# One layer of a hybrid diffusion backbone on one core: scans started one block later, one load per chunk, the gate arithmetic reordered

## The chip, the core and the metric

The kernel runs on one core of a Trainium2 chip: TensorE (PE) for matrix products, VectorE (DVE), ScalarE (ACT) and GpSimd (POOL) for elementwise work, SyncE (SP) as the queue that starts nearly all DMA transfers. Each engine takes its own instructions in order and waits on semaphores for the others. The metric is the device time of one execution in microseconds. Three runs of the kernel before took 1649.82, 1650.39 and 1653.24 us; the median is 1650.39.

## What is computed

The layer takes 1024 latent tokens and 256 context tokens of width 1024. A modulated norm feeds one wide input projection; from it come, for four retention heads and four mLSTM heads, a query, a key, a value and an output gate, further the mLSTM's scalar gates and two wide branch gates. Each head is scanned in both directions, in chunks of 128 tokens:

```python
# retention, one chunk
scores = jnp.einsum("bhld,bhsd->bhls", qc, kc) * intra
out = jnp.einsum("bhls,bhsv->bhlv", scores, vc) + inter[..., None] * jnp.einsum("bhld,bhdv->bhlv", qc, s)
s_new = chunk_decay[:, None, None] * s + jnp.einsum("bhsd,bhsv->bhdv", kc * to_end[..., None], vc)
...
# mLSTM, one chunk: b_cum is the running sum of log forget gates, ic the input gate
log_src = b_last[..., None] - b_cum + ic
m_new = jnp.maximum(b_last + m, jnp.max(log_src, axis=-1))
w_old = jnp.exp(b_last + m - m_new)
w_src = jnp.exp(log_src - m_new[..., None])
c_new = w_old[..., None, None] * c_mat + jnp.einsum("bhs,bhsv,bhsd->bhvd", w_src, vc, kc)
...
y_ret = from_heads(head_norm(ret)).astype(dtype) * jax.nn.silu(rg)
y_ml = from_heads(head_norm(jax.nn.sigmoid(to_heads(mo, ML_HEADS)) * ml)).astype(dtype)
merged = jax.nn.sigmoid(bg_ret) * (y_ret @ w_ret_up) + jax.nn.sigmoid(bg_ml) * (y_ml @ w_ml_up)
x = x + g1 * (merged @ w_out)
x = x + g2 * swiglu(modulate(rms_norm(x, norm2_gain[layer]), sh2, sc2), w_ffn_in[layer], w_ffn_out[layer])
```

All is float32; the kernel writes an operand of a large product as the sum of a high and a low part and adds three products.

## The kernel before

The program is one long pipeline on one core. The part that the change touches is the head section, from about 155 to 776 us of the span. It is a row of 22 blocks (`run_blocks`, L320): `u1p0` to `u7p1` (head u = 1 to 7; part 0 makes its key and value, part 1 its query and gate) and then `bg0` to `bg7` (the branch gates). Every block is a product of 256 by 1024 weights with all 1024 tokens in seven products of half size (`winograd_block`, L276), each of 12 matmuls of 128x512 (`prod`, L253, L258): 84 matmuls. The weights of a block are loaded (L211) and split into high (ACT, L191) and low (DVE, L192) parts one block ahead, after sums and differences on DVE and POOL (L230). Products collect in the PSUM tiles `ch` and `ts`; DVE (L288) or ACT (L286, L293) take them out; the finished tiles are rotated (L576 to L582), stored, or transposed by PE (L564). The first product of a block is issued ahead of the last two of the block before.

Beside the blocks run generators. `tick()` (L994) is called once per product, seven times a block; `beside(gen, rate)` (L1004) adds a generator that is advanced `rate` times per tick on average; `drain()` (L1007) runs all of them to their end. They are:

- `gates()` (L691): the mLSTM's scalar gates for all eight head directions in 36-row tiles `g`: a log-sigmoid by way of DRAM (L706 to L712), six running sums and maxima as DVE scans (L724, L725), sums and differences over 36x1280 elements (L736, L737 on POOL; L741, L747 on DVE), exponentials on ACT (L735, L750, L751), and 30 small PE transposes into `colq` (L768).
- `scan(u)` (L805), one per head. Its steps stand in numbered slots: `load` of a chunk's key and value `kv` from DRAM (L825), `decay` on POOL (L838), `advance` of the running state `sf` or `sb` (PE L852, DVE L857), `load_qk`, and for each of eight output chunks j `stage_a` (L887), `stage_b` (PE L898, DVE L901 or L903) and `stage_c` (PE L915 to L917 or L922 and L923, then ACT L918 or ACT and DVE L925 to L929, POOL L931, and a sum of squares on ACT, L933, whose elementwise result is thrown away in the tile `junk`). `norm_y` (L935) scales, `put_y` (L944) transposes by PE (L947) and stores. The four rotating PSUM buffers `sc` serve all of these.
- `ada2()` (L972): the second modulation vector from 64 loads of 256 KB with one DVE operation each (L983).
- `load_y_ret()` (L1059): loads the retention results for the stage after and splits them (L1069).

What Python issues first does not stand first in the end: a scheduler sets the order of instructions on each engine from the program and the buffers' waits. The rates, slots and buffer counts move it.

## Time and profile before

| what | value |
|---|---|
| median of three runs | 1650.39 us |
| profiled execution, its own time | 1655.51 us |
| its span, first to last instruction | 1653.7 us |
| PE busy | 1578.3 us, 95% |
| DVE busy | 1003.5 us, 61% |
| ACT busy | 725.7 us, 44% |
| POOL busy | 460.2 us, 28% |
| mean granted TensorE clock | 0.984 |

Busy shares are means over very different stages, and a matmul's recorded time covers its way through the array, so that two neighbours overlap. Within the head section a better measure is the length of a block: how long 84 matmuls and the scans' small ones took.

### The profile page before, as it was taken

What the parts mean: (1) busy time and instruction counts of PE and PEld (TensorE: products, weight loads), DVE (VectorE), ACT (ScalarE), POOL (GpSimd) and SP (SyncE); (2) the same over time, 40 slices, a digit from 0 to 9 for tenths busy, and PEclk for the clock granted to TensorE, in tenths of its full rate; (3) what the DMA queues carried; (4) which work ended last, traced back from release to release, by engine and by line L of the source; (5) the groups of instructions that cost most, each with busy time, mean ns of one, the idle gap of its engine ahead of it and who ended that gap; (6) DMA issues with size and microseconds to landing.
All of it is one profiled execution on the core that took longest, in us unless ns stands there. A gap on an engine that the chain in (4) does not pass through costs nothing.

```text
span 1653.7 us, 22635 instructions
## 1 busy us (share of the span) xinstructions
PE 1578.3 (95%) x7478; PEld 1287.9 (78%) x7478; DVE 1003.5 (61%) x1841; ACT 725.7 (44%) x1404; POOL 460.2 (28%) x506
## 2 busy tenths in 40 slices
PE   7999978899999999999999999999999999999997
PEld 2677757787878788778888777888888888888886
DVE  4578786776767767765445677555555555536243
ACT  4655434544545566655223354434443334534230
POOL 0143216455344444410220226222222221001001
PEclk9999978999999999999999999999999999999998
DMA  8753537787767765546456312222232224835531
GB/s 293 255 159 104 167 105 234 252 258 240 248 210 218 228 202 180 187 141 215 154 162 202 122 56 96 81 92 84 85 96 87 77 90 155 271 96 179 171 96 52
DMA packets 188230, 264.55 MB, mean 160 GB/s; under 512 B 19232, under 2 KB 85920, under 8 KB 188112
## 3 DMA queue, kind: packets, MB, share of 16 engines
q1 hardware_dynamic: 186240, 260.99, 49.8%
q10 hardware_dynamic: 1872, 2.10, 0.4%
q8 instruction: 59, 0.97, 0.2%
q14 instruction: 59, 0.48, 0.1%
HBM read 206.64 MB, written 56.38 MB: 159 GB/s over the span
## 4 chain that ended last, share of the span: by engine, by line
PE 51%; POOL 2%; DVE 2%; DMA 1%; ACT 1%; issue 0%; DVEq 0%; SPq 0%; ACTq 0%
PE ch L258 15%; PE ts L258 12%; PE ch L1291 2%; PE ch L1292 2%; PE ch L1290 2%; PE ts L1290 2%; PE ts L1292 2%; PE ts L1291 2%; POOL hid L1158 1%; PE ts L113 1%; PE ch L113 1%; PE ts L112 1%; PE ts L111 1%; PE ch L111 1%; PE ch L112 1%; POOL xf L396 1%
## 5 line engine op out<-in xcount | busy, mean ns | idle before, releaser
L192 DVE TENSOR_TENSOR fw<-raw,fw 128x512 fp32r<-128x512 f32 x305 | 223.1, 737 | 156.6 <-ACT fw L191 156.1
L258 PE MATMUL ts<-A,fw 128*128 128x512 f32 x1200 | 300.7, 398 | 1.8 <-DVE A L397 0.9
L191 ACT CAST fw<-raw 128x512 fp32r<-128x512 f32 x305 | 188.0, 620 | 257.2 <-PE ch L1292 89.0
L258 PE MATMUL ch<-A,fw 128*128 128x512 f32 x1176 | 289.4, 394 | 0.0
L258 PEld LDWEIGHTS ts<-A,fw 128*128 128x128 f32 x1200 | 225.1, 191 | 50.9 <-DVE A L397 3.0
L258 PE MATMUL ch<-t,fw 128*128 128x512 f32 x1008 | 250.4, 396 | 5.5 <-ACT u L293 3.9
L258 PEld LDWEIGHTS ch<-A,fw 128*128 128x128 f32 x1176 | 219.5, 189 | 45.8 <-issue 1.0
L258 PEld LDWEIGHTS ch<-t,fw 128*128 128x128 f32 x1008 | 187.5, 189 | 44.7 <-ACT u L293 5.1
L1158 POOL TENSOR_TENSOR hid<-hid,sg 128x512 f32<-128x512 f32 x44 | 90.2, 2062 | 217.6 <-DVE hid L288 200.9
L258 PE MATMUL ts<-t,fw 128*128 128x512 f32 x504 | 129.6, 404 | 3.2 <-ACT fw L191 1.9
L293 ACT COPY u<-ch 128x512 f32<-128x512 f32 x104 | 60.9, 586 | 134.0 <-PE ch L258 133.7
L258 PEld LDWEIGHTS ts<-t,fw 128*128 128x128 f32 x504 | 95.6, 193 | 23.1 <-ACT fw L191 2.1
L192 DVE TENSOR_TENSOR fw<-stg,fw 128x512 fp32r<-128x512 f32 x126 | 94.5, 750 | 31.3 <-ACT fw L191 31.2
L230 POOL TENSOR_TENSOR stg<-raw,raw 128x512 f32<-128x512 f32 x42 | 63.5, 1513 | 156.2 <-DVE fw L192 100.4
L191 ACT CAST fw<-stg 128x512 fp32r<-128x512 f32 x126 | 78.6, 624 | 59.4 <-DVE stg L230 29.2
L838 POOL TENSOR_SCALAR vs<-kv,dcol 128x128 f32<-128x128 f32 x72 | 63.0, 882 | 63.1 <-DMA kv<-kv_d 33.0
L838 POOL TENSOR_SCALAR vs<-kv,colq 128x129 f32<-128x129 f32 x72 | 54.8, 762 | 78.5 <-PE sc L852 38.0
L1282 POOL TENSOR_SCALAR cp<-cp,cpack 128x256 f32<-128x256 f32 (+1 forms) x6 | 8.2, 1361 | 222.1 <-ACT stg L1336 222.1
L192 DVE TENSOR_TENSOR fw<-s,fw 128x512 fp32r<-128x512 f32 x42 | 33.4, 796 | 48.0 <-ACT fw L191 48.0
L983 DVE SCALAR_TENSOR_TENSOR acc<-stg,silu_c,acc 128x512 f32<-128x512 f32 x56 | 46.8, 836 | 18.2 <-DMA stg<-wada 18.1
L230 DVE TENSOR_TENSOR stg<-raw,raw 128x512 f32<-128x512 f32 x42 | 39.0, 930 | 27.1 <-DMA raw<-wffn 16.8
L396 POOL TENSOR_SCALAR t<-stg,a,sh 128x512 f32<-128x512 f32 (+1 forms) x24 | 27.3, 1144 | 95.8 <-issue 31.5
(362 smaller groups left out, 2973.3 us busy)
## 6 DMA issues: line engine op xcount, KB each, us to landing
raw<-wffn SPq DMA_DIRECT2D x88, 256.0 KB
raw<-wfo SPq DMA_DIRECT2D x88, 256.0 KB
kv<-kv_d SPq DMA_DIRECT2D x152, 128.0 KB
raw<-win SPq DMA_DIRECT2D x64, 256.0 KB
stg<-wada SPq DMA_DIRECT2D x64, 256.0 KB
hid_d<-hid SPq DMA_DIRECT2D x44, 256.0 KB
hraw<-hid_d SPq DMA_DIRECT2D x40, 256.0 KB
araw<-wada SPq DMA_DIRECT2D x32, 256.0 KB
```

The costliest lines, as they stand in the source:

```text
L191: nc.scalar.copy(hi, x)
L192: nc.vector.tensor_tensor(out=lo, in0=x, in1=hi.bitcast(F32), op=ALU.subtract)
L230: eng.tensor_tensor(out=o, in0=x, in1=y, op=op)
L258: nc.tensor.matmul(ps, lhsT=w[wp_][:, c], rhs=x[xp][k], start=start and k == i == 0, stop=cont or (stop and k == 3 and i == 2), skip_group ...
L293: nc.scalar.copy(o, chain)
L396: nc.gpsimd.tensor_scalar(out=tmp, in0=xn, scalar1=scale, scalar2=shift, op0=ALU.mult, op1=ALU.add)
L838: nc.gpsimd.tensor_scalar(out=vs, in0=kv[d, n][1], scalar1=col, scalar2=None, op0=ALU.mult)
L983: nc.vector.scalar_tensor_tensor(out=acc, in0=raw, scalar=s, in1=acc, op0=ALU.mult, op1=ALU.add)
L1158: nc.gpsimd.tensor_tensor(out=c, in0=c, in1=sgs[f, hf], op=ALU.mult)
L1290: nc.tensor.matmul(ps, lhsT=w[0][:, c], rhs=h[0][:, t], start=kt == 0, stop=False)
L1291: nc.tensor.matmul(ps, lhsT=w[0][:, c], rhs=h[1][:, t], start=False, stop=False)
L1292: nc.tensor.matmul(ps, lhsT=w[1][:, c], rhs=h[0][:, t], start=False, stop=kt == 2 * NG - 1)
```

## The change

The generators get other starting places, rates and slots. `gates()` still starts with `u1p0`, now at rate 1.0 and with its steps spread over more yields: the forget gate is loaded and biased first, the log-sigmoid's three DMA trips have yields between them, and the two wide subtractions go from POOL to DVE. The drain, the opening of the scans' pool and `ada2` move from `u2p1` to `u3p0`; `ada2` runs at 0.68 in place of 0.95. `scan(u)` starts with the next head's part 0, at 1.5 slots per tick in place of 1.45, and the last one with `bg4` in place of `bg3`; `load_y_ret` starts with `bg7` at 1.6 in place of `bg6` at 1.0. In a scan each chunk of keys and values is loaded once for both directions (10 loads in place of 19, nine buffers in place of eight), most slots move back by one, `put_y` by two. The mask is loaded by each mLSTM scan into the buffer `dt`, and the sum of squares throws its elementwise result into the last quarter of the PSUM tile `po` in place of `junk`.

```diff
+        def load_rows(t, tl, c0):
+            for x, c in ((t, c0), (tl, c0 + H)):
+                nc.gpsimd.memset(x, 0.0)
+                for d in range(2):
+                    nc.sync.dma_start(x[32 * d:32 * d + H], e_d[c + 32 * d:c + 32 * d + H])
...
+        load_rows(gf, gfl, 64)
+        yield
+        load_rows(gi, gil, 0)
...
+        biased(1, gf, gfl)
         for d in range(2):
             nc.sync.dma_start(rows[0][4 * d:4 * d + H], gf[32 * d:32 * d + H])
         nc.sync.dma_start(lsx, ls_d[0])
         yield
-        log_sigmoid(pg, lso, lsx, [P, 80], "g")
...
+        biased(0, gi, gil)
...
+        yield
+        yield
+        yield
+        log_sigmoid(pg, lso, lsx, [P, 80], "g")
+        yield
...
                 nc.vector.tensor_tensor_scan(out=v(bb), data0=v(rm), data1=v(gf), initial=0.0, op0=ALU.mult, op1=ALU.add)
+                yield
                 nc.vector.tensor_tensor_scan(out=v(m), data0=v(gf), data1=v(gi), initial=m[r, 0:1] if i else 0.0,
                                              op0=ALU.add, op1=ALU.max)
-                yield
-        yield
+                if not (d and i == 0):
+                    yield
...
+        nc.scalar.activation(rm, m, AF.Exp, scale=-1.0)
+        nc.vector.tensor_tensor(out=gi, in0=gi, in1=bb, op=ALU.subtract)
...
+        nc.vector.tensor_tensor(out=bb, in0=bb, in1=m, op=ALU.subtract)
...
-        nc.gpsimd.tensor_tensor(out=gi, in0=gi, in1=bb, op=ALU.subtract)
-        nc.gpsimd.tensor_tensor(out=bb, in0=bb, in1=m, op=ALU.subtract)
...
-        def load(d, n):
-            t = bt([P, 2 * P + 1], "kv", 8)
+        def load(n):
+            t = bt([P, 2 * P + 1], "kv", 9)
...
-            return bt([P, P + 1], "sf", 3)[:, :W]
+            return bt([P, P + 1], "sf", 4)[:, :W]
...
+        for i, n in enumerate((0, 1, 9, 8, 7, 6, 5, 4, 3, 2)):
+            after(i // 2 if i < 9 else 6, load, n)
         for i, n in enumerate((1, 0, 9, 8, 7, 6, 5, 4, 3)):
-            after(i // 2, load, 1, n)
-            at(i // 2 + 2, decay, 1, n)
-            at(i // 2 + 3, advance, 1, n)
-        for n in range(NCH):
-            after(5 + n, load, 0, n)
-            if n < 9:
-                at(7 + n, decay, 0, n)
-                at(8 + n, advance, 0, n)
+            at(i // 2 + 3, decay, 1, n)
+            at(i // 2 + 4, advance, 1, n)
+        for n in range(9):
+            at(4 + n if n < 2 else 7 + n, decay, 0, n)
+            at(6 + n if n < 2 else 8 + n, advance, 0, n)
...
-            junk = bt([P, P], "junk", 1)
-            nc.scalar.activation(junk, raw, AF.Square, accum_out=ssq[:, j:j + 1])
+            nc.scalar.activation(po[:, 3 * P:], raw, AF.Square, accum_out=ssq[:, j:j + 1])
...
-            at(9 + j, stage_a, j)
-            at(10 + j, stage_b, j)
-            at(11 + j, stage_c, j)
-        at(20, norm_y)
-        at(23, put_y, 0)
-        at(24, put_y, 4)
+            at(10 + j, stage_a, j)
+            at(11 + j, stage_b, j)
+            at(12 + j, stage_c, j)
+        at(21, norm_y)
+        at(25, put_y, 0)
+        at(26, put_y, 4)
...
-                if part == 0:
+                if part == 1:
                     return
-                if u == 2:
+                if u == 1:
+                    beside(gates())
+                if u == 3:
                     drain()
                     es_g.close()
                     open_scans()
-                    beside(ada2(), 0.95)
-                if u >= 2:
-                    beside(scan(u - 2), 1.45)
+                    beside(ada2(), 0.68)
+                if u >= 3:
+                    beside(scan(u - 3), 1.5)
...
-                if blk in (1, 3):
-                    beside(scan(2 * H - 2 + blk // 2), 1.45)
-                if blk == 6:
+                if blk in (0, 2, 4):
+                    beside(scan(2 * H - 3 + blk // 2), 1.5)
+                if blk == 7:
                     drain()
                     es_b.close()
-                    beside(load_y_ret())
+                    beside(load_y_ret(), 1.6)
```

Three places show what the scheduler made of it. The first is DVE while `u2p0` runs, around the gate scans. Before, from the last low part of `u1p1` (`fw_1980`) on; `fw_2134` and `fw_2139` are the low parts of `u2p1`'s first two factors, `g` the gate tiles:

```order
L192 TENSOR_TENSOR fw_1980<-raw_1796,fw_1980 128x512
L192 TENSOR_TENSOR fw_2134<-raw_1983,fw_2134 128x512
L230 TENSOR_TENSOR stg_2137<-raw_1985,raw_1987 128x512
L230 TENSOR_TENSOR s_2142<-stg_2137,raw_1983 128x512
L192 TENSOR_TENSOR fw_2139<-stg_2137,fw_2139 128x512
L724 SCALAR_TENSOR_TENSOR g_1576<-g_1575,g_1574 4x1280
L725 SCALAR_TENSOR_TENSOR g_1573<-g_1574,g_1572 4x1280
L724 SCALAR_TENSOR_TENSOR g_1576<-g_1575,g_1574 4x256
L725 SCALAR_TENSOR_TENSOR g_1573<-g_1574,g_1572 4x256
```

The same place now, from behind the six scans (which stand directly above, L740 and L742) to `fw_2062`, the low part of `u2p1`'s first factor; `kt` are finished tiles of `u2p0`:

```order
L755 COPY gm_1549<-g_1543 4x1
L749 TENSOR_TENSOR g_1542<-g_1542,g_1546 36x1280
L756 COPY gm_1549<-g_1543 4x1
L757 COPY gm_1549<-g_1543 4x7
L753 TENSOR_TENSOR g_1546<-g_1546,g_1543 36x1280
L288 TENSOR_TENSOR kt_2027<-ts_2014,u_1916 128x512
L759 TENSOR_TENSOR g_1544<-g_1546,gm_1549 36x1280
L578 TENSOR_TENSOR kt_2027<-kt_2027,rp_2029 128x512
L288 TENSOR_TENSOR kt_2055<-ts_1978,wt_2053 128x512
L579 TENSOR_TENSOR kt_2027<-kt_2027,wt_2033 128x512
L764 COPY gm_1551<-g_1546 4x10 x2
L192 TENSOR_TENSOR fw_2062<-raw_1970,fw_2062 128x512
```

The scans stood behind the first two factors of the next block and now stand ahead of both, with the two subtractions among them.

The second place is PE at the end of `u2p0`. Before, the first gate transpose (L768) stands between the first and the second product of `u2p1`:

```order
L258 MATMUL ch_2155<-A_116,fw_2134 128x512 x2
L258 MATMUL ch_2155<-A_117,fw_2134 128x512
L258 MATMUL ch_2155<-A_116,fw_2134 128x512
L768 MATMUL sc_2071<-cpack,g_1572 128x36 [waits DMAHW2_49,DMAHW4_49,PE_49,Pool_49]
L258 MATMUL ts_2281<-t_1254,fw_2139 128x512 [waits DVE_49]
L258 MATMUL ts_2281<-t_1255,fw_2139 128x512
L258 MATMUL ts_2281<-t_1254,fw_2139 128x512
```

Now, at the same count of large matmuls: `fw_1967` belongs to `u2p0`'s last product, `kt_2055` is the tile that DVE makes above, and `ch_2083` is `u2p1`'s first product, of which two matmuls stand ahead:

```order
L258 MATMUL ch_1903<-A_118,fw_1967 128x512 [waits Activation_49]
L258 MATMUL ch_1903<-A_119,fw_1967 128x512
L258 MATMUL ch_1903<-A_118,fw_1967 128x512 [waits DVE_49]
L258 MATMUL ch_1903<-A_118,fw_1967 128x512
L258 MATMUL ch_1903<-A_119,fw_1967 128x512
L564 MATMUL sc_2098<-cpack,kt_2055 128x128 [waits DVE_49,PE_49]
L564 MATMUL sc_2098<-cpack,kt_2055 128x128 x3
L258 MATMUL ts_1978<-A_118,fw_1964 128x512
L258 MATMUL ts_1978<-A_119,fw_1964 128x512
L258 MATMUL ts_1978<-A_118,fw_1964 128x512 x2
L258 MATMUL ch_2083<-A_116,fw_2062 128x512 [waits DVE_49]
```

The wait for POOL's subtraction is gone from here; the gate transposes (now L782) follow 17 large matmuls and four small ones further on, and a transpose that waits for DVE's `kt_2055` and a matmul that waits for `fw_2062` stand in their place.

The third place is PE in the last mLSTM scan, at two slots in one tick. Before, in `bg4`:

```order
L852 MATMUL sc_7586<-vs_7551,kv_7464 128x129 [waits DMAHW2_49,PE_49,Pool_49]
L922 MATMUL sc_7591<-sf_7508,qs_7517 128x129 [waits DVE_49]
L258 MATMUL ch_7186<-A_118,fw_7303 128x512
L258 MATMUL ch_7186<-A_119,fw_7303 128x512
L923 MATMUL sc_7591<-kv_7444,W_7519 128x129 [waits DVE_49]
L922 MATMUL sc_7591<-sb_7218,qs_7517 128x129
```

Now, in `bg5`:

```order
L936 MATMUL sc_7516<-sf_7404,qs_7430 128x129 [waits DVE_49]
L937 MATMUL sc_7516<-kv_7242,W_7432 128x129 [waits DVE_49]
L936 MATMUL sc_7516<-sb_7121,qs_7430 128x129
L937 MATMUL sc_7516<-kv_7242,W_7432 128x129
L912 MATMUL sc_7529<-qk_7416 128x128 [waits DMAHW2_49,PE_49]
L867 MATMUL sc_7544<-vs_7514,kv_7157 128x129 [waits DVE_49,Pool_49]
L258 MATMUL ts_7592<-t_1254,fw_7370 128x512
L936 MATMUL sc_7549<-sf_7421,qs_7480 128x129 [waits Activation_49]
```

The state `sf_7508` was begun one slot's matmuls ahead of its reader, `sf_7404` now two; and the reader's PSUM buffer is now waited for on ACT.

## Rows read from the trace of the kernel before

**Rows 1.** The page's first part: busy us, share, instructions.
```profile
PE 1578.3 (95%) x7478; PEld 1287.9 (78%) x7478; DVE 1003.5 (61%) x1841; ACT 725.7 (44%) x1404; POOL 460.2 (28%) x506
```
**Rows 2.** Stretches: length, PE busy (matmuls), granted clock, DMA share, GB/s.
```profile
199.64:265.55 65.91, 53.04 (x235) 0.84 0.49 157
265.55:337.26 71.71, 63.31 (x337) 0.93 0.73 232
337.26:737.10 399.84, 380.52 (x2097) 1.00 0.67 210
737.10:756.14 19.04, 19.04 (x85) 1.00 0.64 206
...
424.05:450.37 26.32, 26.32 (x149) 1.00 0.88 278
```
**Rows 3.** PE's waits, 155.15 to 776 us: total us, times, longest.
```profile
PE sc L947 <- DVE o L941: 9.4, 5, 3.5
PE sc L768 <- POOL g L736: 8.9, 1, 8.9
PE sc L922 <- DVE sf L857: 4.7, 4, 2.6
PE sc L915 <- DVE sf L857: 3.6, 3, 1.4
PE sc L852 <- POOL vs L838: 2.6, 2, 2.2
...
PE sc L768 <- ACT g L751: 1.4, 1, 1.4
```
**Rows 4.** PE's waits from 337.26 us on.
```profile
PE sc L947 <- DVE o L941: 5.9, 4, 1.8
```
**Rows 5.** Stretches at low clock: length, busy PE, PEld, DVE, ACT, POOL, clock.
```profile
220.92:231.16 10.24, 5.44 (x13) 4.25 (x14) 10.17 (x10) 3.58 (x5) 7.03 (x3) 0.50 0.03 5
...
237.99:244.82 6.83, 6.83 (x31) 5.59 (x31) 3.23 (x5) 4.16 (x15) 0.00 (x0) 0.50 0.46 125
```
**Rows 6.** PE and POOL in order of time: start, us, what, idle before.
```profile
225.29 0.32 PE L768 MATMUL sc<-cpack,g 36*128 36x36 f32 x1 [8.91 <-POOL g L736]
225.32 2.91 POOL L737 TENSOR_TENSOR g<-g,g 36x1280 f32<-36x1280 f32 x1
```
**Rows 7.** DVE in order of time, in the same stretch.
```profile
211.05 2.81 DVE L724 TENSOR_TENSOR_SCAN g<-g,g 4x1280 f32<-4x1280 f32 x1 [0.23 <-DMA g<-ls_d]
...
222.61 2.65 DVE L732 COPY gm<-g 4x7 f32<-4x7 f32 x1
...
225.90 4.11 DVE L192 TENSOR_TENSOR fw<-s,fw 128x512 fp32r<-128x512 f32 x1
...
231.14 1.48 DVE L741 TENSOR_TENSOR g<-g,gm 36x1280 f32<-36x1280 f32 x1
```
**Rows 8.** The page's costliest groups: busy us, mean ns, idle before.
```profile
L192 DVE TENSOR_TENSOR fw<-raw,fw 128x512 fp32r<-128x512 f32 x305 | 223.1, 737 | 156.6 <-ACT fw L191 156.1
```
**Rows 9.** The gate bias (L703): durations ns, first and last start us.
```profile
L703 DVE SCALAR_TENSOR_TENSOR g<-g,gbias,g x2: 1537/1537/1537, 170.8 to 179.4; 36x1280 f32<-36x1280 f32 x2
```
**Rows 10.** Waits of SP's queue, 155.15 to 776 us: total us, times, longest.
```profile
SPq L825 <- PE sc L852: 22.2, 27, 1.8
...
SPq L758 <- POOL g L737: 14.3, 1, 14.3
```
**Rows 11.** ACT's and POOL's waits, 337 to 737 us.
```profile
ACT junk L933 <- POOL o L931: 17.3, 21, 1.9
...
POOL o L931 <- DVE o L929: 23.7, 15, 4.2
```
**Rows 12.** Durations ns min/median/max of L933 and L931.
```profile
L933 ACT ACTIVATE junk<-o x64: 293/311/323, 279.0 to 714.4; 128x128 f32<-128x128 f32 x64
L931 POOL TENSOR_TENSOR o<-o,g x32: 454/460/892, 511.8 to 713.9; 128x128 f32<-128x128 f32 x32
```
**Rows 13.** DMA issues: number and KB of each.
```profile
kv<-kv_d SPq DMA_DIRECT2D x152, 128.0 KB
```

More of the change, by code (lines that the diff above doesn't have):

```diff
@@ L695, in gates, with biased @@
         ls_d = [dram.tile([P, 80], F32, name=f"ls_d{i}") for i in range(2)]
-        for t in (gi, gil, gf, gfl, bb, mprev):
-            nc.gpsimd.memset(t, 0.0)
-        for t, c0 in ((gi, 0), (gil, H), (gf, 64), (gfl, 64 + H)):
-            for d in range(2):
-                nc.sync.dma_start(t[32 * d:32 * d + H], e_d[c0 + 32 * d:c0 + 32 * d + H])
-        yield
-        for i, (t, tl) in enumerate(((gi, gil), (gf, gfl))):
-            nc.vector.scalar_tensor_tensor(out=t, in0=t, scalar=gbias[:, i:i + 1], in1=tl, op0=ALU.add, op1=ALU.add)
-        rows = [ls_d[i].rearrange("(r q) c -> r (q c)", q=16) for i in range(2)]
+        rows = [ls_d[i].rearrange("(r q) c -> r (q c)", q=16) for i in range(2)]
+        def load_rows(t, tl, c0):
[3 more added lines that the diff above has]
+                    nc.sync.dma_start(x[32 * d:32 * d + H], e_d[c + 32 * d:c + 32 * d + H])
+        def biased(i, t, tl):
+            nc.vector.scalar_tensor_tensor(out=t, in0=t, scalar=gbias[:, i:i + 1], in1=tl, op0=ALU.add, op1=ALU.add)
+        load_rows(gf, gfl, 64)
+        yield
+        load_rows(gi, gil, 0)
+        nc.gpsimd.memset(bb, 0.0)
+        nc.gpsimd.memset(mprev, 0.0)
+        yield
+        biased(1, gf, gfl)
         for d in range(2):
@@ L708, in gates @@
         yield
-        log_sigmoid(pg, lso, lsx, [P, 80], "g")
-        nc.sync.dma_start(ls_d[1], lso)
-        for d in range(2):
-            nc.sync.dma_start(gf[32 * d:32 * d + H], rows[1][4 * d:4 * d + H])
+        biased(0, gi, gil)
         m, rm = gil, gfl
@@ L717, in gates @@
         nc.gpsimd.memset(rm[32:36, P - 1::P], 0.0)
+        yield
[3 more added lines that the diff above has]
+        yield
+        nc.sync.dma_start(ls_d[1], lso)
+        for d in range(2):
+            nc.sync.dma_start(gf[32 * d:32 * d + H], rows[1][4 * d:4 * d + H])
+        yield
+        yield
         yield
@@ L783, in open_scans @@
         t = {}
-        t["mask"] = pb.tile([P, 2, P], F32, name="mask")
-        nc.sync.dma_start(t["mask"], a["mask"])
         t["g128"] = pb.tile([P, 2, H], F32, name="g128")
@@ L810, in scan @@
         slots, ends = {}, {}
-        g128, mask = held["g128"], held["mask"]
+        g128 = held["g128"]
         if ret:
             dt_, dec, dcol = decay_tables(h)
+        else:
+            mask = bt([P, 2, P], "dt", 1)
+            nc.sync.dma_start(mask, a["mask"])
         def at(slot, fn, *args):
@@ L851, in advance @@
             ps = sc_ps()[:, :W]
-            nc.tensor.matmul(ps, lhsT=kv[d, n][0], rhs=vsd.pop((d, n)), start=True, stop=True)
+            nc.tensor.matmul(ps, lhsT=kv[n][0], rhs=vsd.pop((d, n)), start=True, stop=True)
             if old is None:
@@ L910, in stage_c @@
             raw = ot[j // 4][:, j % 4, :]
[L911 removed]
+            v = kv[n][1]
             sf, sbj = state[0, n - 1], sb[:, j, :W]
@@ L1022, in first @@
             def first():
-                if (u, part) == (1, 0):
-                    beside(gates(), 0.85)
-                if part == 0:
+                if part == 1:
                     return
-                if u == 2:
+                if u == 1:
+                    beside(gates())
+                if u == 3:
                     drain()
```

29 lines of the change are left out of this document (13 added, 16 removed).

## The prediction

> **What bounds the kernel now.** I read the page's totals first: PE is busy for 1578.3 us [rows 1] of a span of 1653.7 (own time 1655.51), so DVE, ACT and POOL matter where PE stands still for them, or where its clock drops. The totals don't say where. For that I cut the head section into stretches of whole blocks, since every block is the same 84 matmuls [rows 2], and ask what each stretch costs above its work. The price of a bare block is the last group of the first four stretches: `bg6`, in which no scan runs, took 19.04 us (one of its 85 matmuls reaches in from the edge; each stretch has such a one). The price of a small scan matmul follows from `bg4`, the row below it: 26.32 us for 149, so (26.32 − 19.04) / 64 = 0.114 us. Then, of [rows 2]:
>
> - A, `u2p0` and `u2p1`: 65.91 − 2 × 19.04 − 66 × 0.114 = 20.3 us in excess
> - B, `u3p0` and `u3p1`: 71.71 − 38.08 − 168 × 0.114 = 14.4
> - C, the 14 blocks `u4p0` to `bg5`: 399.84 − 266.56 − 920 × 0.114 = 28.4
>
> Together 63 us are there to win. The list of PE's waits [rows 3] comes next, then the stretches at low clock [rows 5], because a wait can cost twice: once itself, and once by what follows at half speed. Last come POOL, DVE and SP in order of time, where the waits lead [rows 6, 7, 10].
>
> **A: the gate arithmetic.** PE stood 8.91 us before its first gate transpose for POOL's first subtraction, ending at 225.3, and POOL's second took another 2.91 us [rows 6]. With 0.4 behind the second, 1.4 behind ACT's exponential and 2.2 behind the first decay's `vs` these are 12.9 us [rows 3]. Twice PE then ran at a granted clock of 0.50, 1.2 instead of 2.4 GHz, first behind the long wait and then behind the sparse stretch that followed it; PE was busy for 5.44 and 6.83 us there [rows 5], of which half, 6.1, would not have been needed at full clock. 19.0 of the 20.3 us have a name.
>
> The change takes the subtractions off PE's way: the transposes stand 17 large matmuls later and POOL isn't in the chain. What is late next? PE now stops for DVE's `kt_2055` and `fw_2062`, both queued behind the six scans and the subtractions. I place DVE's work by the old times. Bias of the forget gate: it was second, at 179.4, and becomes first, at 170.8 [rows 9]; 8.6 us earlier. If the DMA trips behind it follow, the first scan starts at 211.05 − 8.6 [rows 7], about 203 with half a us of spare. Scans and copies lasted from 211.05 to 222.61, 11.6 us [rows 7]. Ahead of `kt_2055` three 36x1280 operations are added, and I price them at the 1.48 us of L741, the same shape on DVE [rows 7], and four 128x512 operations at the 0.74 of L192 [rows 8]: 203 + 11.6 + 4.4 + 3.0 = 222.0; `fw_2062` comes 1.7 us behind (two such and the small copies). PE, which reached its old stop at 225.29 − 8.91 = 216.4, meets the new one five large matmuls (0.227 us each, 19.04 / 84) earlier, at 215.25. It waits 6.75 us, runs four small matmuls, and waits 0.8 more: 7.5. One slow stretch then follows as before, 2.7, and the 1.3 unexplained stays: 11.5 of 20.3 remain, **gain 8.8**. Bounds: 0, if the scans come as late as before, and 20.3, if DVE has done all before PE asks.
>
> The last low part that DVE did beside POOL's subtraction took 4.11 us [rows 7] against a mean of 0.74 [rows 8], so POOL also cost DVE 3.4 us there; as DVE operations the two subtractions cost 3.0. By that row alone the move is an even trade for DVE; for the chain it replaces 5.8 us of POOL (two of 2.91) by 3.0.
>
> The Trainium skill ("SBUF — State Buffer", "Who interferes with whom") says that a DVE instruction with two SBUF inputs contends with a GpSimd instruction that reads SBUF, and one with at most one input outside the two-port modes does not. The 4.11 us of the two-input L192 agree. By the rule the one-input copy of 4x7 elements would have cost the same without POOL beside it, and the sum would put 2 us more into the new wait; the trace gives that copy 2.65 us [rows 7], which is long for 28 elements, so I leave the sum as it is.
>
> **B: the first scan.** 0.07 × 71.71 = 5.0 us is clock (0.93 [rows 2]). 3.5 us is the wait of the transposes in `put_y` for the scaled `o` (9.4 in all less 5.9 from 337.26 on [rows 3, 4]). SP's queue had stood 14.3 us for POOL's second subtraction [rows 10], and all loads queued behind it came in a burst. The change starts this scan a block after the gates, ends that wait, and puts one more slot between `norm_y` and `put_y`. I let the wait for `o` go, the clock's loss fall to 1, and 5.4 of the other 5.9 stay: **gain 8**. Bounds 0 and 14.4.
>
> **C: the steady scans.** PE waits for `o` 5.9 us, at most 1.8 at once [rows 4]. A tick is a seventh of a block, 399.84 / 98 = 4.08 us. The distance from `norm_y` to `put_y` goes from 3 / 1.45 = 2.07 ticks to 4 / 1.5 = 2.67, 2.4 us more than now: longer than the longest wait, so I count **5** of 5.9. The wait of an output for its running state `sf` is 4.7 + 3.6 = 8.3 us, at most 2.6 [rows 3]; the state is now made two slots' order earlier in place of one, 1.38 to 2.0 ticks, 2.5 us more. I count **6** of 8.3. The rest of C's 28.4, spread over hundreds of short stops, stays; bounds of C are 0 and 28.4. What comes next behind those waits is PE's PSUM buffer, under D.
>
> **D: what the change adds.**
> - The sum of squares (L933) now writes into `po`, so an `sc` buffer is free only when ACT has done it; before, for mLSTM, it was free behind DVE's last read. Per place this is 0.46 for POOL's product and 0.31 for the square [rows 12], and their waits (23.7 + 17.3) / 32 = 1.28 [rows 11]: 2.05 us. There are 32 mLSTM places; with four buffers most are asked for later than that. In the new order of PE's instructions I count 13 places where the buffer is asked for again with few large matmuls between. All 13 lost would be 27, all 32 lost 66, none 0. The row nearest is the wait of 23.7 that POOL already has without PE standing still for it, so I take 2 places fully late: **−4**.
> - Ninth `kv` buffer, but a chunk held for both directions: SP's queue waits for a free one behind `advance`'s PE matmul 27 times, 22.2 us, longest 1.8 [rows 10]. Eight of these exposed at 1.8 would be 14, none 0; loads come several slots ahead, I take **−1**.
> - `load_y_ret` starts a block later: eight splits of 0.74 us on DVE [rows 8] in 7 ticks, 6 of 19 us, beside DVE work of the last block; the stage after waits for the last one. Bounds 0 and 8, **−1**.
> - 72 fewer loads of 128 KB (152 before [rows 13]) run at a DMA share of 0.67 in C [rows 2]: nothing, as no PE wait in [rows 3] is for `kv`; if the queue was what kept `vs` late, the 2.2 of [rows 3] return, counted in A. The mask loads (one per mLSTM scan), `ada2` at the lower rate and the later scans move work that PE doesn't wait for; PE's own matmuls are the same in number.
>
> **Sum.** 8.8 + 8 + 5 + 6 − 4 − 1 − 1 = 21.8 us; 1655.51 − 21.8 = 1633.7 by the profiled execution, which lies 5.1 above the median of the runs: **1628** as a median.
>
> **Rivals.**
> 1. *The square keeps PSUM.* If PE asks for an `sc` buffer within 2.05 us of DVE's last read at more than two places in three of the 32, the cost is 22 × 2.05 = 45, more than all gains (27.8 − 2). At 13 exposed places 27 are lost against 25.8 gained: from here on it is slower. At 16, 33 − 26 = 7 slower: 1657. For it: ACT and POOL already wait for each other there [rows 11]. Against: none of the releasers in [rows 3] is the last reader of an `sc` buffer, so PE has not stood for a free one so far. Chance 0.12.
>    The Trainium skill ("PSUM — Partial Sum Buffer", "PSUM bank collisions raise a hardware error") says that accesses of different engines to a bank must be ordered, so that ACT's write keeps PE's next matmul out of the whole buffer, its other quarters too. No row of before shows this, since the squares went to SBUF.
> 2. *The gate chain doesn't come earlier.* The log-sigmoid has more yields now, at 1.0 step per tick; if the scans start at 211 as before, `fw_2062` is done at about 232 and A's gain is gone, and B's clock stays low behind it: 11 − 6 = 5 gained, 1645. For it: the scans waited 0.23 us for a DMA [rows 7], so the trips set their start. Chance 0.16.
> 3. *Everything goes.* DVE is through before PE asks, the clock stays up in A and B, and C's two waits go: 20 + 12 + 14 − 4 = 42, with D at 0 47: 1608 to 1603. For it: 8.6 us of head start is as much as the wait that I leave. Chance 0.12.
> 4. *The tail.* The up projection waits for `load_y_ret` the full 8 us: 1636. Chance 0.07.
>
> **How the numbers follow.** The forecast has 0.53; its own range is 1615 to 1640 (A 0 to 15, C 5 to 14, D 0 to −10). Each rival keeps its chance. The range reaches half way into rivals 1 and 3: 1608 to 1652. A measurement of this kernel can tell about 0.2%, 3.3 us, from no change: faster means below 1647, and takes the forecast, rivals 3 and 4, and rival 2 but for 0.04: 0.84. Rival 1 is slower except where just 12 or 13 places are exposed: 0.10. The same time 0.06.
>
> **What would show it.** A is right if PE's wait before the gate transposes is gone and in its place stand waits for DVE's `kt` (L288) and `fw` (L192) of 6 to 8 us together, with one stretch at 0.50 instead of two in the first scan blocks; it is wrong if the first scan starts after 208 in the old time. B: the mean clock of the first scan's two blocks is 0.98 or more. C: PE's wait at the `put_y` transposes for DVE's `o` is under 1 us, that for `sf` under 2.5. D: PE waits on ACT's square under 4 us. If the sum of PE's waits on the square passes 26 us, the forecast falls with rival 1.

## The result, and the profile after

The changed kernel took 1643.68 us (median of five runs, 1640.53 to 1645.44) against 1652.39 of the kernel before (five runs, 1649.82 to 1653.24): ratio 0.994, interval [0.9925, 0.9955], 8.7 us faster. The forecast was 22 us faster: the side was right and the time stood inside the wide range (1608 to 1652), but outside the forecast's own (1615 to 1640), and the gain was 0.4 of the one forecast. The time lies next to rival 2's 1645, but not for rival 2's reason: there the gate chain comes no earlier, and here the first of the gate scans on DVE started at 204.67 us (shown below) in place of 211.05 [rows 7].

The profiled execution took 1645.44 us, 10.07 less than the one of before. Its first part, against [rows 1]: PE's busy time fell by 4.7 us, DVE's by 7.7 and POOL's by 11.8 (38 operations fewer); ACT's rose by 1.1.

```profile
PE 1573.6 (96%) x7478; PEld 1283.3 (78%) x7478; DVE 995.8 (61%) x1843; ACT 726.8 (44%) x1406; POOL 448.4 (27%) x468
```

The stretches of [rows 2] in the changed kernel: A, B, C and `bg6` (length, busy PE, PEld, DVE, ACT, POOL, clock, DMA share, GB/s).

```profile
200.12:255.41 55.29, 44.91 (x215) 36.04 (x214) 45.43 (x56) 24.66 (x49) 14.59 (x10) 0.91 0.54 160
255.41:318.41 63.00, 56.94 (x293) 47.63 (x292) 39.60 (x83) 31.25 (x72) 30.10 (x32) 0.95 0.71 223
318.41:722.61 404.20, 387.27 (x2141) 328.47 (x2140) 287.74 (x674) 219.61 (x510) 176.31 (x266) 1.00 0.64 194
722.61:744.04 21.43, 21.22 (x102) 17.40 (x100) 11.47 (x29) 11.69 (x22) 0.00 (x0) 1.00 0.57 189
```

The lengths can't be compared directly, because a block's worth of scan matmuls has moved from A and B to C and `bg6`. The excess can (length less 19.04 a block, less 0.114 per small matmul, as in the prediction): A 12.0, B 10.8, C 27.7, `bg6` 0.5. So A gave 8.3 us, B 3.6, C 0.7; `bg6` and the two blocks ahead of A took back 1.4. The head section ends 12.1 us earlier (763.86 against 775.98). Behind it 2.1 us were lost again, 1.3 of them in a dip of the clock near 1010 us, with PE busy for 5.99 us in place of 3.41 at 0.50 (half of the difference), in a stage that the change doesn't touch:

```profile
1008.71:1015.53 6.82, 5.99 (x14) 4.72 (x15) 3.88 (x7) 3.01 (x6) 0.00 (x0) 0.50 0.42 115
```

PE's waits in the head section, 155 to 764 us, against [rows 3]:

```profile
PE ch L258 <- ACT wt L293: 9.6, 1, 9.6
PE sc L867 <- DVE wt L964: 4.6, 2, 3.7
PE sc L929 <- DVE sf L872: 3.0, 5, 1.2
PE sc L931 <- DVE W L915: 2.6, 5, 1.8
PE sc L867 <- POOL vs L853: 2.5, 3, 1.8
PE sc L867 <- DVE sf L872: 2.5, 3, 2.1
...
PE sc L960 <- DVE o L954: 0.5, 3, 0.2
...
PE sc L936 <- ACT sc L946: 0.2, 1, 0.2
```

The two waits that the slots were to end did end: for the scaled `o` 9.4 became 0.5, for the state `sf` 8.3 became 3.0. In their place PE waits at `advance` (L867) for PSUM buffers that DVE has not emptied yet, 7.1 us (4.6 and 2.5); the same line's 2.6 of before (L852) were for `vs`. That these waits took the place of the others is a reading of the two lists. The square (L946) is hardly in the list.

The stop in `u2p0`, PE, DVE and ACT in order of time:

```profile
204.67 2.81 DVE L740 TENSOR_TENSOR_SCAN g<-g,g 4x1280 f32<-4x1280 f32 x1
...
213.72 0.61 PE L258 MATMUL ch<-A,fw 128*128 128x512 f32 x2
215.45 2.34 DVE L742 TENSOR_TENSOR_SCAN g<-g,g,g 4x1024 f32<-4x1024 f32 x1
217.83 1.27 ACT L748 ACTIVATE g<-g 36x1280 f32<-36x1280 f32 x1 [8.76 <-DVE g L742]
221.35 0.68 DVE L288 TENSOR_TENSOR kt<-ts,u 128x512 f32<-128x512 f32 x1
222.06 0.62 ACT L574 COPY wt<-kt 64x512 f32<-64x512 f32 x1 [2.96 <-DVE kt L288]
223.33 0.58 ACT L293 COPY wt<-ch 128x512 f32<-128x512 f32 x1
223.97 2.50 PE L258 MATMUL ch<-A,fw 128*128 128x512 f32 x5 [9.64 <-ACT wt L293]
```

Read upwards: PE wants a `ch` buffer, ACT's copy empties it, ACT stands in its order behind a rotation copy, this behind DVE's `kt`, this behind the scans and subtractions. DVE's lump of gate work is still what stops PE, by way of another engine's queue, and for 9.64 us, longer than the 8.91 of [rows 6].

### The profile page after: what moved, and what is told of

Same layout as the page of the kernel before. It is cut to its first block, busy times and chain, and to the rows that moved or that the text cites. A ratio compares the mean times of both kernels' runs of the same rounds, so it can differ in the third digit from the quotient of the medians.

```text
span 1643.7 us, 22385 instructions
## 1 busy us (share of the span) xinstructions
PE 1573.6 (96%) x7478; PEld 1283.3 (78%) x7478; DVE 995.8 (61%) x1843; ACT 726.8 (44%) x1406; POOL 448.4 (27%) x468
## 5 line engine op out<-in xcount | busy, mean ns | idle before, releaser
L258 PE MATMUL ts<-A,fw 128*128 128x512 f32 x1200 | 296.8, 394 | 2.7 <-DVE kt L288 1.0
L258 PEld LDWEIGHTS ts<-A,fw 128*128 128x128 f32 x1200 | 221.4, 188 | 50.8 <-DVE A L397 3.0
L258 PE MATMUL ch<-t,fw 128*128 128x512 f32 x1008 | 254.2, 400 | 5.3 <-ACT u L293 3.7
L258 PE MATMUL ts<-t,fw 128*128 128x512 f32 x504 | 124.9, 394 | 0.0
L853 POOL TENSOR_SCALAR vs<-kv,dcol 128x128 f32<-128x128 f32 x72 | 55.3, 778 | 52.9 <-PE sc L867 35.4
L853 POOL TENSOR_SCALAR vs<-kv,colq 128x129 f32<-128x129 f32 x72 | 51.1, 718 | 55.5 <-PE sc L867 41.5
L867 PE MATMUL sc<-vs,kv 128*128 128x128 f32 (+1 forms) x288 | 48.4, 284 | 10.5 <-DVE wt L964 4.6
L867 PEld LDWEIGHTS sc<-vs,kv 128*128 128x128 f32 x288 | 42.2, 193 | 16.9 <-DVE wt L964 5.4
```

The lines of the kernel that those rows point to most:

```text
L258: nc.tensor.matmul(ps, lhsT=w[wp_][:, c], rhs=x[xp][k], start=start and k == i == 0, stop=cont or (stop and k == 3 and i == 2), skip_group ...
L853: nc.gpsimd.tensor_scalar(out=vs, in0=kv[n][1], scalar1=col, scalar2=None, op0=ALU.mult)
L867: nc.tensor.matmul(ps, lhsT=kv[n][0], rhs=vsd.pop((d, n)), start=True, stop=True)
```

## The experiments

Ratios are to the kernel before, run on the same chip in five rounds, with 95% intervals. A, B and C are the excess in us, cut from each run's own trace in the same way; each is one execution, and a stretch of 3.41 us at a clock of 0.50 more or less moves one by up to 1.7 us. Several experiments ran on different chips, so differences between two of them are taken from the ratios.

| kernel | ratio | A | B | C |
|---|---|---|---|---|
| before | 1 | 20.3 | 14.4 | 28.4 |
| changed | 0.9940 [0.9925, 0.9955] | 12.0 | 10.8 | 27.7 |
| square_to_sbuf | 0.9931 [0.9914, 0.9949] | 12.1 | 10.8 | 27.7 |
| ada2_fast | 0.9956 [0.9939, 0.9973] | 12.0 | 10.4 | 31.3 |
| slots_back | 1.0017 [1.0004, 1.0030] | 12.1 | 12.5 | 40.0 |
| gates_only | 0.9945 [0.9928, 0.9961] | 13.7 | 12.2 | 28.3 |
| gates_slots | 1.0000 [0.9985, 1.0014] | 13.1 | 10.8 | 35.9 |
| kv_twice | 0.9932 [0.9912, 0.9953] | 12.0 | 6.6 | 32.3 |
| rate_145 | 0.9948 [0.9930, 0.9966] | 12.3 | 11.2 | 27.5 |
| scans_early | 0.9950 [0.9934, 0.9966] | 12.4 | 14.2 | 24.9 |
| old_gates | 0.9947 [0.9928, 0.9966] | 16.3 | 8.7 | 27.7 |
| sub_on_pool | 0.9965 [0.9951, 0.9978] | 18.0 | 12.0 | 28.7 |
| gates_slots_kv9 | 0.9976 [0.9960, 0.9991] | 12.6 | 8.8 | 35.5 |
| no_ada2 | 0.9840 [0.9818, 0.9863] | 11.3 | 7.4 | 21.2 |
| puty_alone | 0.9914 [0.9901, 0.9928] | 13.1 | 10.1 | 22.5 |
| before_no_ada2 | 0.9905 [0.9892, 0.9918] | 18.3 | 10.7 | 26.1 |
| ada2_part_ffn | 0.9932 [0.9917, 0.9947] | 11.1 | 7.9 | 27.2 |
| ada2_behind_scans | 0.9933 [0.9921, 0.9945] | 11.1 | 7.8 | 27.5 |
| puty_ada_slow | 0.9969 [0.9951, 0.9987] | 12.6 | 9.8 | 34.0 |
| puty_ada_ffn | 0.9973 [0.9960, 0.9987] | 14.0 | 11.9 | 33.5 |

**square_to_sbuf**, the prediction's first rival:

```diff
-            nc.scalar.activation(po[:, 3 * P:], raw, AF.Square, accum_out=ssq[:, j:j + 1])
+            junk = bt([P, P], "junk", 1, mybir.dt.bfloat16)
+            nc.scalar.activation(junk, raw, AF.Square, accum_out=ssq[:, j:j + 1])
```

> The changed kernel with one line back: the sum of squares throws its elementwise result into an SBUF tile again (in bf16, for room) and not into po. Theory 1 (the square holds the PSUM buffers: the new wait of PE at advance, 12 us of excess in the 14 steady blocks, is due to it): 6 to 9 us faster than the changed kernel's 1643.7, ratio to before about 0.989, and the waits at advance fall below 5 us. Theory 2 (the square is hidden; advance waits because DVE and ACT empty the buffers late): within 2 us of the changed kernel, ratio 0.993 to 0.995, waits at advance stay at 10 us or more.

Nothing moved: the time is the same within the intervals, the excess within 0.1 us. That is theory 2's side. The rival and the 4 us of the forecast's D fall.

**ada2_fast**:

```diff
-                    beside(ada2(), 0.68)
+                    beside(ada2(), 0.95)
```

> The changed kernel with the second modulation at its old rate of 0.95 in place of 0.68. Theory A (the spread modulation lets DVE stand for its loads until bg6, and PE behind it, in the mLSTM scans; it is what ate the gain): 3 to 8 us faster than 1643.7, ratio 0.989 to 0.992, PE's waits from bg0 on shorter by 3 us or more. Theory B (its DVE work is in nobody's way at either rate): within 2 us. Theory C (the lower rate is a gain: denser DVE work delays the early scans): 3 us or more slower, in the blocks u3p0 to u7p1.

2.6 us slower by the ratios, whose intervals overlap, and C 3.6 higher: it leans to theory C. Theory A, that the spread ate the gain, is not borne out.

**slots_back**, the output stages and `put_y` as before:

```diff
-            at(10 + j, stage_a, j)
+            at(9 + j, stage_a, j)
...
-        at(21, norm_y)
-        at(25, put_y, 0)
-        at(26, put_y, 4)
+        at(20, norm_y)
+        at(23, put_y, 0)
+        at(24, put_y, 4)
```

> The changed kernel with the output stages one slot earlier and put_y two slots earlier, as before the change: the state has two slots to its reader again, the scaled o three to its transposes. Theory 1 (the two waits that the longer distances remove are real gains): 8 to 11 us slower than 1643.7, about 1653, with 5 us of wait at the put_y transposes and 8 us at the reader of sf. Theory 2 (the waits only moved to advance, for whose buffers they now compete): within 3 us of 1643.7, and PE's excess at advance falls from 12 us to under 7 while the other two come back.

12.7 us slower, more than theory 1 gave, but not by its waits. In this arrangement the later outputs and `put_y` together are thus worth 12.7 us. PE's waits in C:

```profile
PE sc L912 <- DVE sf L872: 8.3, 6, 2.1
PE sc L867 <- DVE sf L872: 4.8, 3, 1.7
...
PE sc L960 <- DVE o L954: 0.7, 1, 0.7
```

The wait for `o` hardly came back, and the outputs' products wait for `sf` 1.6 us in place of the expected 8; `stage_b`'s product (L912) now waits for a PSUM buffer that `advance`'s DVE operation empties. In the changed kernel the backward advances stand a slot later too; that the outputs, moved forward again, fall among them is how I read it, and no run shows it by itself.

**gates_only**, the kernel before with the new body of `gates()`:

```diff
-                    beside(gates(), 0.85)
+                    beside(gates())
```

> The kernel before with only the new body and rate of the gate generator; scans, slots, buffers and the second modulation as before. Forecast's own reasoning: about 8 us of wait and clock in u2p0 and u2p1 go, ratio 0.994 to 0.996, so that nearly all of the change's measured gain of 8.7 us is this. Rival (the gates' gain needs the scans to start a block later, since the first scan's decay waits for the gate results' loads): the stop moves to u2p1, under 3 us gained, ratio 0.998 or more.

9.1 us faster: as the forecast's reasoning said, and as much as the whole change within the noise. The stop, 9.6 us, is there as in the changed kernel.

**gates_slots**: on top of it the later outputs and `put_y`, four `sf`, the square in `po`:

```diff
-            return bt([P, P + 1], "sf", 3)[:, :W]
+            return bt([P, P + 1], "sf", 4)[:, :W]
...
-            at(9 + j, stage_a, j)
+            at(10 + j, stage_a, j)
...
-        at(23, put_y, 0)
+        at(25, put_y, 0)
```

> The kernel before with the new gates (0.9945 alone) and, of the rest, only the output stages one slot later, put_y two later, the fourth sf buffer and the square into po; loads, starts and rates as before. Theory 1 (the longer distances are worth the 11 us that the forecast gave them in the steady blocks, and another part eats them): 8 to 11 us faster than the gates alone, ratio 0.988 to 0.990, and put_y's waits for o and the readers' waits for sf go without a new wait at advance. Theory 2 (the waits only move to the advances and their buffers): within 3 us of the gates alone, ratio 0.993 to 0.996, with advance waiting 8 us or more.

Neither: all of the gates' gain is lost, C goes from 28.3 to 35.9.

**kv_twice, rate_145, scans_early**: the changed kernel with one part back each, the loads with their advance slots, the rate, or the starts.

```diff
+        for i, n in enumerate((1, 0, 9, 8, 7, 6, 5, 4, 3)):
+            after(i // 2, load, 1, n)
+            at(i // 2 + 2, decay, 1, n)
+            at(i // 2 + 3, advance, 1, n)
```
```diff
-                    beside(scan(u - 3), 1.5)
+                    beside(scan(u - 3), 1.45)
```
```diff
-                if u >= 3:
-                    beside(scan(u - 3), 1.5)
+                if u >= 2:
+                    beside(scan(u - 2), 1.5)
```

> The changed kernel with each chunk's keys and values loaded once for each direction again, and the decay and advance slots that belong to it as before; nine buffers. Theory S (sharing the loads put the backward advances a slot later, under the last head's put_y, and this costs what the distances gain): 5 to 9 us faster than the changed kernel, ratio 0.9885 to 0.991, waits at advance for the put_y copies gone. Theory N (loads and their slots are worth nothing either way): within 2 us, 0.9925 to 0.9955. Theory G (the saved loads are a gain, for SP's queue is what holds the decays up): 3 us or more slower.

> The changed kernel with the scans at 1.45 slots per tick in place of 1.5. Theory D (the denser slots are what makes PE wait at advance): 3 to 6 us faster. Theory N: within 2 us. Theory P (the scans then end later, and put_y reaches into bg6 and bg7 and the next scan's output stages): 2 us or more slower.

> The changed kernel with all scans, the drain and the second modulation a block earlier, where they were before. Forecast's reasoning (the later start is needed so that the first scan doesn't meet the gates): 3 to 6 us slower than the changed kernel, in u2p1 to u3p1. Rival (the gates are through early enough, the start is worth nothing): within 2 us. In the steady blocks both expect the same waits as in the changed kernel.

All three lie within 2 us of the changed kernel: alone, none of the three is worth anything that shows in the time. By the traces two of them move excess from one stretch to the other: kv_twice has 4.2 us less in B and 4.6 more in C, scans_early 3.4 more in B and 2.8 less in C.

**old_gates**, the changed kernel with the old `gates()` at 0.85:

> The changed kernel with the old body and rate of the gate generator (both subtractions on POOL, input gate first, fewer yields); all else as changed. Theory 1 (the gates are the whole gain, and the rest of the change is worth nothing by itself): 7 to 10 us slower than the changed kernel, ratio to before 0.998 to 1.001. Theory 2 (the parts overlap: with the scans a block later the old gates' wait is partly hidden): 3 to 6 us slower, ratio 0.996 to 0.998.

Only 1 us slower: nearest to theory 2, and below its 3 us. Gates alone 9.1 us, all but the gates 8.8, both together 9.9. By the table the two overlap in A (6.6 and 4.0 alone, 8.3 together) and in B (2.2 and 5.7, 3.6 together). In A and B of old_gates:

```profile
199.25:258.99 59.74, 47.80 (x216) 38.04 (x215) 49.34 (x61) 25.05 (x50) 16.91 (x10) 0.89 0.41 127
258.99:319.99 61.00, 55.15 (x294) 46.61 (x293) 42.65 (x85) 30.40 (x70) 33.51 (x34) 0.97 0.79 246
...
PE sc L768 <- POOL g L736: 9.1, 1, 9.1
```

and of gates_only:

```profile
199.99:259.61 59.62, 49.40 (x238) 39.06 (x236) 44.66 (x60) 26.92 (x52) 17.80 (x16) 0.91 0.58 182
259.61:328.66 69.05, 61.70 (x334) 52.23 (x332) 53.99 (x104) 33.52 (x76) 41.83 (x42) 0.95 0.78 241
...
PE ch L258 <- ACT wt L293: 9.6, 1, 9.6
```

Each keeps a stop of over 9 us and the 10.24 us at a clock of 0.50 that go with it; what shrinks is what came later. The kernel before has two more stretches at 0.50 in A, of 6.83 [rows 5] and of 3.42 us:

```profile
261.88:265.30 3.42, 3.42 (x10) 2.65 (x9) 1.01 (x2) 0.00 (x0) 1.58 (x2) 0.50 1.07 384
```

In old_gates one of 3.41 us is left of them, in gates_only and in the changed kernel none, and the mean clock of A rises from 0.84 to 0.89 and 0.91. What follows the stop can be saved only once: that is how I read the overlap in A; what overlaps in B no run parts.

**sub_on_pool**, the changed kernel with both subtractions back:

```diff
-        nc.vector.tensor_tensor(out=gi, in0=gi, in1=bb, op=ALU.subtract)
+        nc.gpsimd.tensor_tensor(out=gi, in0=gi, in1=bb, op=ALU.subtract)
```

> The changed kernel with only the two wide subtractions back on POOL. Forecast's reasoning (the transposes stand later and PE's new stop hangs on DVE's scans, so that POOL's 5.8 us come in the way again only in part): 2 to 4 us slower, in u2p0 and u2p1. Rival 1 (the subtractions are the gain): 6 us or more slower. Rival 2 (the order and the earlier bias are the gain; DVE is relieved of 3 us that stand before the tiles PE waits for): within 2 us or faster, with PE's wait in u2p0 down from 9.6 to 7 us.

4 us slower by the ratios, whose intervals just overlap, as the forecast's reasoning said. The trace has it in A: 18.0 against 12.0, with stops of 8.3 and 4.0 us in place of the one of 9.6. But the traced execution took 1654.24 us, while the other eleven lie between 1646.32 and 1648.99, so that the 18.0 is more than the usual. Within the new order the subtractions belong on DVE: with them on POOL it is no better than the old order (0.9965 against 0.9947).

**gates_slots_kv9**, gates_slots with nine `kv` buffers:

```diff
-            t = bt([P, 2 * P + 1], "kv", 8)
+            t = bt([P, 2 * P + 1], "kv", 9)
```

> The kernel before with the new gates, the later output slots and a ninth kv buffer (the mask loaded per scan into dt, for room); it differs from the run with eight buffers (ratio 1.000) by that. Theory K (the later slots hold each chunk a slot longer, and eight buffers then made SP and the decays late: the ninth is what the slots need): 5 to 8 us faster than with eight, ratio 0.994 to 0.997. Theory L (it is the phase of the scans against one another, at 1.45 and these starts): within 2 us of it, 0.9985 to 1.0015.

4 us faster than with eight, by ratios whose intervals just overlap: between theory L's 2 and theory K's 5, and neither is shown. C stays at 35.5.

**no_ada2**:

```diff
-                    beside(ada2(), 0.68)
+                    nc.vector.memset(mod2, 0.0)
```

> The changed kernel without the second modulation: its 64 loads and 64 DVE operations are left out and the vector is zero. Theory V (what remains of PE's waits in the steady blocks is DVE coming late, in its order, to the tiles that PE waits for and to the PSUM buffers that it empties; 48 us of DVE work and 20 us of its waits for loads go): PE's excess in the 14 blocks from u4p0 on falls from 28 us to under 18, the head ends 8 to 14 us earlier, ratio 0.985 to 0.989. Theory W (the four PSUM buffers and the chain of a chunk set the waits, whatever DVE does beside): under 4 us faster than the changed kernel.

16.5 us less than the changed kernel (0.984 against 0.994), more than theory V's 8 to 14. C is 392.32 us long against 404.20; its excess falls to 21.2, not under 18, since 47 small matmuls went as well. They are the part of the second modulation that the expectation leaves out: PE adds up its products in 64 matmuls of 128x1, in eight groups, each with one of the `sc` buffers. In the changed kernel, and one such group between the large matmuls of ada2_behind_scans (below):

```profile
L1001 PE MATMUL sc<-ones,acc x64: 165/250/250, 314.8 to 735.7; 128*128 128x1 f32 x64
...
775.66 0.95 PE L1001 MATMUL sc<-ones,kt 128*128 128x1 f32 x8
776.47 0.48 PE L111 MATMUL ts<-yr,fw 128*128 128x512 f32 x1
```

A group takes PE 0.81 us (775.66 to 776.47), so the eight are about 6.5 us of PE's own time, an estimate from this row; PE's busy time fell by 6.2. Some 10 of the 16.5 us remain for DVE's work, the loads and the buffers together, and the run does not part these.

**puty_alone**, gates_only and one slot for `put_y`:

```diff
-        at(23, put_y, 0)
-        at(24, put_y, 4)
+        at(24, put_y, 0)
+        at(25, put_y, 4)
```

> The kernel before with the new gates (0.9945) and, of the slots, only put_y one slot later; nothing else. Theory 1 (a wait is worth its own length, as the forecast priced it): the 9.4 us of waits for the scaled o go and the ratio falls by 0.004 to 0.006, to 0.989 to 0.9905. Theory 2 (what PE waits for next in the same slot comes nearly as late, from the same DVE queue): the waits for o go, but PE's excess in u4p0 to bg5 stays within 3 us of 28.5, ratio 0.993 to 0.996.

Nearest to theory 1, though 0.9914 is short of its 0.989 to 0.9905: 5.1 us by the ratios. In C the excess fell from 28.3 to 22.5, as much as the wait for `o` there (5.9 in gates_only, 0.2 now). Its C and PE's waits there:

```profile
327.12:721.08 393.96, 380.48 (x2097) 323.16 (x2096) 281.32 (x665) 216.45 (x506) 169.62 (x288) 1.00 0.69 214
...
PE sc L937 <- DVE W L917: 3.4, 9, 0.6
PE sc L936 <- DVE sf L871: 3.2, 4, 1.4
PE sc L929 <- DVE sf L871: 2.9, 2, 2.0
...
PE sc L961 <- DVE o L955: 0.2, 1, 0.2
```

The same place in gates_slots_kv9, which differs by the outputs one slot later (with the fourth `sf`, the ninth `kv`, the square in `po` and the mask per scan):

```profile
324.07:732.45 408.38, 386.20 (x2110) 325.33 (x2108) 283.94 (x669) 225.34 (x513) 172.63 (x289) 0.99 0.67 209
...
PE sc L938 <- DVE W L918: 5.4, 7, 1.3
PE sc L913 <- DVE sf L872: 3.4, 4, 1.2
...
PE sc L932 <- DVE W L916: 2.2, 2, 1.9
PE sc L930 <- DVE sf L872: 2.2, 2, 1.3
...
PE sc L867 <- ACT sc L947: 1.1, 1, 1.1
```

The readers of `sf` wait 2.2 us in place of 6.1. The waits for `W`, shown here, are 7.6 in place of 3.4, and those for PSUM buffers 4.5 (L913, and L867 behind the square). C is 14.4 us longer and has 13.0 us more excess. Of these 9.0 are listed waits (22.1 us in all, with those not shown, against 13.1); one more stretch of 3.41 us at a clock of 0.50 is up to 1.7; the rest sits in stops too short for the list.

puty_alone, 1638.03 us, is clearly faster than the kernel before. Its ratio is 0.0026 below that of the changed kernel, measured on another chip, with intervals that just overlap: that it beats the changed kernel is likely and not shown.

**before_no_ada2**, the same edit in the kernel before:

> The kernel before without the second modulation: its 64 loads and 64 DVE operations are left out and the vector is zero. Theory V (DVE's lateness sets the excess of the scan blocks in both kernels): 12 to 20 us faster, ratio 0.988 to 0.9925, and the waits for o and sf fall without any slot moved. Theory W (the distances set it in the kernel before; DVE's load matters only in the changed one): under 8 us faster, ratio over 0.995, the waits for o and sf at 15 us or more as before.

15.7 us less, within theory V's 12 to 20; about 6.5 of it are again PE's own 64 matmuls. Waits for `o` fell from 9.4 to 4.5 and for `sf` from 8.3 to 4.0 with no slot moved. Both are waits for DVE's results, so that DVE's load is likely behind half of them; but the loads and the turns in the `sc` buffers went too, and no run takes away DVE's part alone.

**ada2_part_ffn** and **ada2_behind_scans**, complete kernels with that work elsewhere:

```diff
+    beside(ada2((6, 7), lambda: acc2), 0.2)
+    run_blocks(seven_blocks, tick)
...
+    beside(ada2(range(2, 6), head_tile), 1.3)
```

> The changed kernel, complete, with the last quarter of the second modulation (two of its eight column blocks, needed only at the very end) beside the feed-forward blocks, and the other six in the head section at 0.51 in place of 0.68. Theory V (each of its steps costs PE about 0.26 us in the scan blocks: 17 us for 64): 20 steps fewer there, 3 to 5 us faster than the changed kernel, ratio about 0.9915; the feed-forward stage no longer. Rival (only the last few steps in a tick count, spreading them is enough or PE pays in the feed-forward stage): within 2 us, 0.993 to 0.995.

> The changed kernel, complete, with only two column blocks of the second modulation beside the scans (rate 0.17), four beside the up projection and two beside the feed-forward blocks. Theory V: three quarters of the 17 us, 10 to 13 us faster than the changed kernel, ratio 0.986 to 0.988, if the up projection, whose PE never waits, takes 4 x 8 DVE steps of 0.75 us for nothing. Rival (the up projection loses them again: its loads already hold the DMA queues at a share of 0.64): under 5 us faster, 0.991 or more, the loss seen in the 87 us of the up projection.

Both rivals: 1 us each. Theory V's price of 0.26 us a step (17 us for 64) holds PE's own matmuls too, and those move with the work. In the second the head section ends 9.6 us earlier (754.25 against 763.86), and the up projection gives most of it back; the same 384 matmuls of the changed kernel and of this one:

```profile
764.09:852.36 88.27, 88.27 (x385) 71.91 (x384) 41.31 (x64) 19.99 (x34) 20.02 (x15) 1.00 0.56 179
```
```profile
754.48:849.37 94.89, 93.69 (x416) 76.55 (x415) 67.75 (x100) 19.67 (x34) 21.59 (x15) 0.98 0.78 254
```

**puty_ada_slow**, puty_alone with the second modulation at 0.68 (its twin, puty_ada_ffn, has six column blocks beside the scans at 0.51 and two in the feed-forward stage):

> The kernel before with the new gates, put_y one slot later (0.9914 with these two) and the second modulation at 0.68 in place of 0.95. If the gains add: 2 to 4 us faster than without the lower rate, ratio 0.989 to 0.990. If they overlap: within 2 us, 0.990 to 0.9928. If the modulation now reaches into scans that it had left alone: slower, 0.993 or more.

9 us slower than puty_alone, on another chip, with intervals well apart: the third of the expected cases. C rises from 22.5 to 34.0, and the readers of `sf` wait 9.5 us in place of 6.1. The lower rate, in the changed kernel a gain of 2.6 us if it is one, costs over three times that here. The twin, puty_ada_ffn, was expected 3 to 5 us faster than puty_alone if the gains add; it too is 10 us slower.

## Why the prediction was wrong in size

- **A, 8.8 forecast, 8.3 measured.** Right in size, in part by luck. The stop stood not at `kt_2055` and `fw_2062` (7.5 forecast) but a product earlier, at a `ch` buffer behind ACT (9.64, and 0.7 at a `kt` later): I followed DVE's queue to its readers, not into the queue of the engine that reads them. The clock then cost 1.5 us (half of the 3.08 that PE was busy at 0.50) in place of the 2.7 and the unexplained 1.3 of the forecast. That 1.3 was a third stretch at 0.50, 261.88 to 265.30, which the prediction's "twice" left out. Now there is one in place of three. The forecast's wait was too short by 2.8 and its clock cost too long by 2.5.
- **B, 8 forecast, 3.6 measured.** The clock's mean is 0.95, not 0.98. The wait for `o` went, but `put_y`'s PSUM buffer then kept `advance` for 3.7 us, just inside C.
- **C, the step that failed.** "I count **6** of 8.3" took the listed wait for `sf` as time to be had, and D took the loads, the lower rate of `ada2` and the later scans at nothing, as "work that PE doesn't wait for". The wait for `sf` did fall, to 3.0, and C came out at 0.7 in place of 11 less 4. The runs show that the slots have no price of their own. At the old starts, loads and rates the outputs' shift and what came with it cost 10 us (0.9914 to 0.9976; C from 22.5 to 35.5), where I had booked a gain of 6. In the changed arrangement the later outputs and `put_y` are worth 12.7 us (slots_back; C 40.0 against 27.7). And the rest of the change, most of which I took at nothing, costs C 11.7 us where the slots are the old ones (slots_back's 40.0 against 28.3 in gates_only); the lower rate of `ada2` alone costs 9 us behind puty_alone. In the changed kernel slots and rest cancel. The other half of the term, 5 for `put_y`, was right by itself: 5.1.
- **D.** The square: 0 in place of 4. The loads, the rate and the later starts: nothing each that shows in the time when they are taken back one by one, but not nothing together, as said under C. The tail: nothing in place of 1.
- **The sum.** It added terms that overlap: gates and the rest are worth 9.1 and 8.8 alone and 9.9 together.
- **Open.** Why the later outputs cost 10 us at the old starts, loads and rates and not at the new. That a later output is also a later request for `W` and for PSUM buffers, among other advances, agrees with the waits of gates_slots_kv9, and no run shows it by itself. kv_twice, rate_145, scans_early and ada2_fast change one part each, and none brings the cost back; combinations of them were not run.

## What to carry to other kernels

A wait on PE's list names what came last; before its length is booked as a gain, look at what the same group of instructions needs next, the buffers to be emptied among it, and who empties them. Moving one consumer that nothing else follows (`put_y`) returned its wait in C (5.8 us of excess for 5.9 of wait); moving a whole stage with its producers and buffers cost 10 us in one arrangement and was part of a gain of 12.7 in another. So price a move in the arrangement in which it will stand, and don't take the other moved parts at nothing because PE doesn't wait for them now. Two edits that each end the aftermath of the same stop are worth it once: price the aftermath by itself. And when work is left out to find its price, count first what of it runs on the engine that bounds the kernel.
